# A short first load ahead of 64 KB runs in a streaming loss kernel

## The chip, the cores and the metric

The kernel runs on one core of one Trainium2 chip. The metric is the device time of one execution in microseconds. The profile's own span is some 1.3 us shorter (82.9 against 84.23 in the profiled run of the kernel before).

## The reference

```python
batch, dim = 1024, 4096            # log_input and target, float32
loss = np.exp(log_input) - target * log_input
return np.mean(loss, axis=-1).astype(np.float32)
```

Two inputs of 16.8 MB each are read once, and 4 KB are written.

## The kernel before

Partition p holds rows 8p to 8p+7, so eight rows of one partition lie one after another in HBM, 128 KB in all. ScalarE (ACT) does the exp with its row sum, VectorE (DVE) the product with its row sum, and all loads are issued by the sync engine (SP). The first load takes four rows of x at once: 128 runs of 64 KB, eight on each of the 16 transfer engines.

```python
    loads = []
    for first, rows in ((0, 4), (4, 2), (6, 1)):
        loads += [("x", first * d, rows * d), ("t", first * d, rows * d)]
    # ... the last row follows in seven ever smaller loads (TAIL)

    for i, (what, lo, w) in enumerate(loads):
        if what == "x" and lo in (6 * d, 7 * d):
            free = 1 if lo == 6 * d else 4
            nc.sync.wait_ge(exp_done, free)      # rows 6 and 7 reuse the first buffer
            nc.sync.wait_ge(prod_done, free)
        src = x_v if what == "x" else t_v
        dma = nc.sync.dma_start(out=place(what, lo, w), in_=src[:, lo : lo + w])
        dma.then_inc(landed[i] if i < len(loads) - 1 else last_ready, 16)
        if lo < 6 * d:
            early.append(dma.ins)
    before_first_barrier(nc, early)              # the first four issues go ahead of the barrier
```

Each load counts its semaphore up by 16, once per transfer engine, and the computing engines wait for 16. ACT starts when the first x load has landed, DVE when the first t load has.

## Time and profile before

| | before |
|---|---|
| device time, median of 3 | 84.14 us (83.91 to 84.20) |
| span of the profile | 82.9 us |
| HBM read | 33.55 MB, 405 GB/s over the span |
| first x load landed, first t load landed | 22.08 us, 41.41 us |
| DVE busy, ACT busy | 43%, 40% |

The transfers are the bound: DVE and ACT are idle more than half the time, and the last landing is followed only by about 2 us of computing and output. The page counts packets by size:

```profile
DMA packets 2016, 33.56 MB, mean 405 GB/s; under 512 B 352, under 2 KB 608, under 8 KB 1120
```

The second, of the timeline, is the exp table load, with its start, its length, and in brackets its wait:

```profile
2.97 1.28 ACT L155 ACT_TABLE_LOAD   x1 [2.97 <-PEq L48]
```

### The profile page before, as it was taken

Reading aid. Unit: us, or ns where it says so; the run is one execution under the profiler, and the core shown is the slowest. Engines: PE = TensorE matmul, PEld = TensorE weight load, DVE = VectorE, ACT = ScalarE, POOL = GpSimd, SP = SyncE. Lnnn points to the kernel's source line nnn. Section 1 sums busy time; section 2 is a strip of 40 time slices with the busy share of each in tenths; the row PEclk is TensorE's granted clock in tenths of the full one; section 3 lists DMA queues with packets and bytes.
Section 4 is the critical chain, followed back from the end, with each engine's and each line's share of the span. In section 5 each row is a group of like instructions: output and inputs, shape, how many; then the busy total and the mean of one; then the engine's idle time right before and its main releaser. Section 6 shows DMA issues by size and latency. Waiting matters only on the chain.

```text
span 82.9 us, 131 instructions
## 1 busy us (share of the span) xinstructions
DVE 35.6 (43%) x22; ACT 33.2 (40%) x35; POOL 0.3 (0%) x5
## 2 busy tenths in 40 slices
DVE  0000000000000000000099999999469996994992
ACT  0500000000399920000000897979793496019460
POOL 0000000000000000000000000000000000000000
DMA  9199999929999992999699799899899999999950
GB/s 506 63 443 506 506 506 506 443 127 443 506 506 506 506 443 127 443 506 506 269 490 474 316 474 490 380 411 490 364 403 435 443 435 393 433 397 421 393 184 2
DMA packets 2016, 33.56 MB, mean 405 GB/s; under 512 B 352, under 2 KB 608, under 8 KB 1120
## 3 DMA queue, kind: packets, MB, share of 16 engines
q1 hardware_dynamic: 2016, 33.56, 95.5%
HBM read 33.55 MB, written 0.00 MB: 405 GB/s over the span
## 4 chain that ended last, share of the span: by engine, by line
DMA 72%; DVE 18%; issue 4%; SPq 3%; ACT 1%
DMA t_big<-in_target_dram 49%; DMA x_big<-in_log_input_dram 23%; DVE t_big L175 17%; SPq L129 3%; DVE t_big L193 1%; ACT e_dump L155 1%; DVE parts L175 0%; SPq L127 0%; DVE all_loss L193 0%
## 5 line engine op out<-in xcount | busy, mean ns | idle before, releaser
L175 DVE CUSTOM_DVE_ANT_0 t_big<-t_big,x_big 128x4096 f32<-128x4096 f32 (+2 forms) x8 | 26.2, 3306 | 43.8 <-DMA t_big<-in_target_dram 43.6
L155 ACT ACTIVATE e_dump<-x_big 128x4096 f32<-128x4096 f32 (+3 forms) x8 | 21.8, 2730 | 24.2 <-DMA x_big<-in_log_input_dram 24.0
L175 DVE CUSTOM_DVE_ANT_0 t_mid<-t_mid,x_mid 128x4096 f32<-128x4096 f32 x2 | 8.8, 4424 | 2.0 <-DMA t_mid<-in_target_dram 2.0
L141 ACT ACTIVATE join_dump<-parts 128x2 f32<-128x2 f32 x7 | 1.4, 203 | 20.4 <-DVE parts L175 20.4
L155 ACT ACTIVATE e_dump<-x_mid 128x4096 f32<-128x4096 f32 x2 | 7.1, 3568 | 0.0
L155 ACT ACT_TABLE_LOAD x1 | 1.3, 1283 | 3.0 <-PEq L48 3.0
L155 ACT ACTIVATION_READ_ACCUMULATOR e_dump<-x_big 128x1 f32 x8 | 1.5, 186 | 0.0
L141 ACT ACTIVATION_READ_ACCUMULATOR join_dump<-parts 128x1 f32 x7 | 1.3, 186 | 0.0
L193 DVE CUSTOM_DVE_ANT_0 t_big<-t_big,x_big 128x390 f32<-128x390 f32 x1 | 0.6, 566 | 0.1
L175 DVE DVE_READ_ACCUMULATOR2_ANT parts<- 128x1 f32 x7 | 0.6, 81 | 0.0
L155 ACT ACTIVATION_READ_ACCUMULATOR e_dump<-x_mid 128x1 f32 x2 | 0.4, 186 | 0.0
L175 DVE DVE_READ_ACCUMULATOR2_ANT t_big<- 128x1 f32 x3 | 0.2, 83 | 0.0
L136 POOL MEMSET x_big<- 128x6 f32 x1 | 0.1, 103 | 2.5 <-POOLq L48 2.5
L227 POOL MEMSET const-bfloat16-1.0<- 128x1 bf16 x1 | 0.1, 101 | 0.0
L227 POOL MEMSET const-uint8-127<- 128x1 uint8 x1 | 0.1, 101 | 0.0
L227 POOL MEMSET const-float32-0.0<- 128x1 f32 x1 | 0.1, 98 | 0.2 <-issue 0.2
L227 POOL MEMSET const-float32-1.0<- 128x1 f32 x1 | 0.1, 98 | 0.0
L193 DVE DVE_READ_ACCUMULATOR2_ANT all_loss<- 128x1 f32 x1 | 0.1, 84 | 0.0
## 6 DMA issues: line engine op xcount, KB each, us to landing
x_mid<-in_log_input_dram SPq DMA_DIRECT2D x1, 4096.0 KB, 50.2
t_mid<-in_target_dram SPq DMA_DIRECT2D x1, 4096.0 KB, 59.5
x_big<-in_log_input_dram SPq DMA_DIRECT2D x1, 2048.0 KB, 19.8
t_big<-in_target_dram SPq DMA_DIRECT2D x1, 2048.0 KB, 24.3
x_big<-in_log_input_dram SPq DMA_DIRECT2D x1, 1536.0 KB, 15.3
t_big<-in_target_dram SPq DMA_DIRECT2D x2, 768.0 KB, 17.6
x_big<-in_log_input_dram SPq DMA_DIRECT2D x1, 384.0 KB, 18.8
t_big<-in_target_dram SPq DMA_DIRECT2D x1, 320.0 KB, 19.1
```

The lines of the kernel that those rows point to most:

```text
L129: dma = nc.sync.dma_start(out=place(what, lo, w), in_=src[:, lo : lo + w])
L136: nc.gpsimd.memset(big["x"][:, 4 * d : 4 * d + n_parts], -1.0).then_inc(ones_done, 1)
L141: nc.scalar.activation(out=join_dump[:, 2 * row : 2 * row + 2], in_=parts[:, 2 * row : 2 * row + 2], func=ACT_F.Copy, scale=inv_d, accum_o ...
L155: nc.scalar.activation(out=e_dump[:, col : col + w], in_=place("x", lo, w), func=ACT_F.Exp, bias=0.0, scale=1.0, accum_out=parts[:, 2 * ro ...
L175: nc.vector.tensor_tensor_reduce(out=place("t", lo, w), in0=place("t", lo, w), in1=place("x", lo, w), scale=-1.0, scalar=0.0, op0=ALU.mult ...
L193: nc.vector.tensor_tensor_reduce(out=place("t", lo, w + n_parts), in0=place("t", lo, w + n_parts), in1=place("x", lo, w + n_parts), scale= ...
L227: nc = _bacc.Bacc("TRN2", target_bir_lowering=False, num_devices=1)
```

## The change

The intent is to let the transfers start on something short: the first 256 columns (1 KB per partition, 128 KB in all) come by a load of their own, and a second load brings the remaining 63 KB of each 64 KB run. Both count up the same semaphore, so its users wait for 32.

```diff
+FIRST = 256
+    full = [32] + [16] * (len(loads) - 2)
-        dma = nc.sync.dma_start(out=place(what, lo, w), in_=src[:, lo : lo + w])
-        dma.then_inc(landed[i] if i < len(loads) - 1 else last_ready, 16)
-        if lo < 6 * d:
-            early.append(dma.ins)
+        sem = landed[i] if i < len(loads) - 1 else last_ready
+        cuts = [lo, lo + FIRST, lo + w] if i == 0 else [lo, lo + w]
+        for a, b in zip(cuts, cuts[1:]):
+            dma = nc.sync.dma_start(out=place(what, a, b - a), in_=src[:, a:b])
+            dma.then_inc(sem, 16)
+            if lo < 6 * d:
+                early.append(dma.ins)
 # ... and three waits on landed[...] take full[...] in place of 16
```

More of the change, by code (lines that the diff above doesn't have):

```diff
@@ L161 @@
             accum_out=parts[:, 2 * row : 2 * row + 1] if row < last_row else part(k - last_row),
-        ).wait_op(landed[i], 16, "sem-ge").then_inc(
+        ).wait_op(landed[i], full[i], "sem-ge").then_inc(
             exp_done if k < n_x - 1 else last_ready, 1
@@ L172 @@
         if j == 0 or x_load > t_work[j - 1][2]:
-            nc.vector.wait_ge(landed[x_load], 16)
+            nc.vector.wait_ge(landed[x_load], full[x_load])
         if j < n_t - 1:
@@ L185 @@
                 else part(n_x - last_row + j - last_row),
-            ).wait_op(landed[i], 16, "sem-ge").then_inc(
+            ).wait_op(landed[i], full[i], "sem-ge").then_inc(
                 prod_done if j < n_t - 2 else last_ready, 1
```

## The prediction

> **What bounds the kernel now.** I read the chain of waits first, because it says what the end hangs on; then the waits in order of cost; then the bytes and the busy share of the transfer engines in stretches that follow the landings; and last, in narrow stretches, the first ten microseconds, where the change acts.
>
> The page of the kernel before opens with the span, and its chain says what ended last:
>
> ```profile
> span 82.9 us, 131 instructions
> DVE 35.6 (43%) x22; ACT 33.2 (40%) x35; POOL 0.3 (0%) x5
> DMA 72%; DVE 18%; issue 4%; SPq 3%; ACT 1%
> HBM read 33.55 MB, written 0.00 MB: 405 GB/s over the span
> ```
>
> Both compute engines are busy under half of the span, and the chain is 72% transfer. 33.55 MB have to come in. What the chain's 18% of DVE hides is seen in its pieces in order of time, start and length first:
>
> ```profile
> 0.43 40.99 DMA t_big<-in_target_dram
> 41.44 4.42 DVE t_big L175
> 59.00 0.33 SPq L129
> 61.30 18.97 DMA x_big<-in_log_input_dram
> 80.28 0.02 issue
> 80.82 0.02 issue
> 80.84 0.57 DVE t_big L193
> ```
>
> The pieces from 41.44 to 59.00 are there only because the issue of the tail loads waits for a buffer; the queue is not empty meanwhile, as the next view shows. It cuts the span at the landings of the first x load (22.08), the first t load (41.41) and the middle t load (60.85); the last three columns are clock, busy share of the 16 transfer engines, and GB/s:
>
> ```profile
> 0.00:22.08 22.08, 0.00 (x0) 1.28 (x1) 0.30 (x5) 1.00 1.02 427
> 22.08:41.41 19.33, 0.00 (x0) 7.42 (x4) 0.00 (x0) 1.00 0.94 409
> 41.41:60.85 19.44, 17.47 (x8) 13.60 (x15) 0.00 (x0) 1.00 1.00 430
> 60.85:80.75 19.90, 17.55 (x12) 10.83 (x16) 0.00 (x0) 1.00 0.95 395
> ```
>
> A packet is booked where it starts, so shares lean between neighbours; the durations are the firmer reading. The first four rows of t, 8.39 MB, need 19.33 us (434 GB/s). The first four rows of x, the same bytes on an idle machine, land at 22.08, that is 2.75 us more. The stream never runs dry afterwards, and from the last landing only about 2 us of compute and output follow. So the end is: start-up of the transfers, plus 33.55 MB at the pace of the slowest transfer engine, plus a fixed tail. The change can only touch the first of these three.
>
> Where the 2.75 us go, by narrow stretches at the start, each of which holds the starts of 16 packets of 64 KB, one per transfer engine, or none:
>
> ```profile
> 0.90:1.70 0.80, 0.00 (x0) 0.00 (x0) 0.00 (x0) 1.00 3.97 1311
> 1.70:3.90 2.20, 0.00 (x0) 0.93 (x1) 0.10 (x1) 1.00 0.00 0
> 3.90:4.90 1.00, 0.00 (x0) 0.36 (x1) 0.00 (x0) 1.00 2.42 1049
> 4.90:6.30 1.40, 0.00 (x0) 0.00 (x0) 0.00 (x0) 1.00 0.00 0
> 6.30:7.30 1.00, 0.00 (x0) 0.00 (x0) 0.00 (x0) 1.00 2.42 1049
> ```
>
> Share times width, times 16 engines over 16 packets, is the mean time of one packet: 3.97 x 0.80 = 3.18 us in the first round, 2.42 x 1.00 = 2.42 us in the second and third. So the first round costs 0.76 us per engine above pace, and the first packets begin about 1.0 us after the first issue. 1.0 + 0.76 = 1.76 us; the last engine of the second round begins at about 4.83 where the mean is about 4.37, so another 0.45 us is the lag of one straggler, which it carries to the end because every engine then runs at one pace. 1.0 + 0.76 + 0.45 plus the spread of the first starts (the last at 1.64, mean 1.19, so 0.2 for the mean) is 2.4; the rest, about 0.35, is from the last byte to the landing seen by the waiter.
>
> [...] the first issue ends at 0.38 and packets begin at 1.0, so 0.62 us. [...] In the stretch 79.0 to 79.2, in the small tail loads, the trace has 73 packets (10 of them semaphore writes) at 377 GB/s with a busy share of 1.08, so 349 GB/s of busy time against 434 for 64 KB packets. [...]
>
> **The change part by part.**
> (1) Added: one more issue, 0.43 us on the sync engine's queue like its neighbours, before the first barrier. The later early issues move by 0.45 to 0.5 us (0.43 plus the 0.05 gap). The second t load is needed on the engines only at 21 us, so this is hidden. The barrier also moves, and with it the exp table load, now 2.97 to 4.25; its first user starts at 22.1. Nothing on the path.
> (2) Added: 128 packets of 1 KB, 8 on each engine. 131 KB at 349 GB/s are 0.375 us, where they took 131 KB / 434 = 0.302 us inside the long runs: +0.07 us on the path. One more semaphore write per engine is about 0.01.
> (3) Moved: the long runs shrink to 63 KB, 8 of them at 27.1 GB/s are 19.04 us instead of 19.33 us.
> (4) Moved: the start-up. First bytes flow where the first packet's end lies 2.42 us away: mean 4.35 - 2.42 = 1.93 us. The small packets are then written by about 1.93 + 0.375 = 2.3. The second load's descriptors come 0.47 us after the first's, so its reads begin at about 1.19 + 0.47 = 1.66 and, if they too need the full 0.76, give data at 2.42; if the path is warm by then, before 2.3. So the long runs flow from 2.3 to 2.42, where before the same byte flowed at 1.93 + 0.30 = 2.23. Sum of (2) to (4) for the mean engine: +0.07 to +0.19 us.
> (5) Moved: the straggler. The end is not that of the mean engine but of the last, 0.45 us behind. [...] I take half of the lag off as my central guess: about -0.25 us. That is a choice, not a reading.
> Center: +0.1 - 0.25 = -0.15 us, about 84.0 us.
>
> **The rivals.** First, that the 0.76 us are the crowding of sixteen 64 KB reads that start together, and not a latency. For it: engines that start late in the first round (1.62 and 1.64) are not late in the second. If small packets get through quickly and stagger the engines, the second load's first round is at pace and up to 0.35 us (all that its 0.47 us later start leaves: 1.66 against 1.19 + 0.76 + 0.07 is 0.36) comes off the mean engine, with the straggler 0.8 us: 83.3 us. Second, that the first long packet pays the 0.76 us in any case and the small load only stands ahead of it with a bubble: +0.2 us and a new straggler of the same size, 84.3 to 84.5 us. For it: the fill is paid per first 64 KB packet, and only 0.37 us of work lies ahead to hide it. Third, that nothing at the start counts since compute sets the end. Against it: the last x landing releases ACT at 80.30 and the last compute runs at 80.84, 0.1 us behind its data; a start-up gain passes through one to one. Fourth, a shift into the tail: tail loads are issued from 59.00 to 62.2 and reach the engines only at about 70, so even 1 us less start-up leaves no hole there.
>
> **Range and chances.** The whole that can be moved is 0.76 + 0.45 = 1.2 us, 1.4% of 84.14, so over 2% (1.68 us) faster would need more than all of it, and slower by 2% has no cause in sight: one issue and 0.07 us of packet cost. The three runs of before span 0.3 us, which I add on both sides. Predicted 84.0 us, 83.3 to 84.5 for 8 in 10; faster 3%, within 96%, slower 1%.
>
> **What would show it.** Right: the first x load complete at 21.6 to 22.2 us, the t load exactly 19.3 us behind it, the barrier and table load some 0.45 us later with nothing following from it, 144 more packets under 2 KB (128 of data and 16 semaphore writes), and unchanged 2.42 us rounds less 1/64. The first rival is right if the long packets' first round is at pace (2.38 us); the second if its mean is 3.1 us again. Wrong altogether: if the distance between the x and the t landing changes, as then the change acts on the steady pace, which I hold impossible; or if the first four rows land more than 1.2 us earlier, as then the 0.62 us before the first packet also depends on the size.

## The result, and the profile after

| | before | after |
|---|---|---|
| device time, median of 6 runs each | 84.06 us (83.91 to 84.20) | 84.19 us (84.04 to 84.50) |
| ratio | | 1.0018, interval 0.9996 to 1.0039 |
| the change again (6 and 11 runs) | 83.96 us | 84.31 us, ratio 1.0044, interval 1.0021 to 1.0068 |

A ratio is the mean time of one kernel's runs over that of the other's in the same rounds, so it is not quite the ratio of the two medians. Executions over 1.5% slower than the fastest of the same kernel are left out of the means. The difference is far under 2%. Taking both together, the change costs 0.2 to 0.4%, some 0.15 to 0.35 us; only the second interval stands clear of 1. A ratio of 1.0012 to 1.003 was expected, or 0.9993 to 1.0007 if there was no cost; 1.0044 lies above both.

The profile after is that of an 84.50 us run, the slowest of the six, 0.31 us above their median. Its span and packet count, of the page:

```profile
span 83.2 us, 132 instructions
...
DMA packets 2160, 33.56 MB, mean 404 GB/s; under 512 B 368, under 2 KB 752, under 8 KB 1264
```

Its table load, of the timeline:

```profile
3.43 1.28 ACT L163 ACT_TABLE_LOAD   x1 [3.43 <-PEq L52]
```

And pieces of its chain of waits in order of time (start, length):

```profile
0.90 40.81 DMA t_big<-in_target_dram
...
41.73 4.43 DVE t_big L183
...
61.62 18.92 DMA x_big<-in_log_input_dram
80.54 0.02 issue
...
81.11 0.57 DVE t_big L201
```

There are 144 packets more, all of them under 2 KB. The barrier and with it the table load moved by 0.46 us, which matters to nobody. The t landing, and everything in the chain behind it, moved by 0.3 us from 41.41 to 41.71, and the last compute by the same 0.27 us from 80.84 to 81.11. So nothing was gained or lost between 41 us and the end; the whole of this difference arises before the first t load has landed.

Stretches at the start of the same profile (from:to, width, busy time of the engines, clock, busy share of the 16 transfer engines, GB/s):

```profile
0.90:1.49 0.59, 0.00 (x0) 0.00 (x0) 0.00 (x0) 1.00 0.57 165
1.49:2.60 1.11, 0.00 (x0) 0.00 (x0) 0.00 (x0) 1.00 2.83 960
4.40:5.40 1.00, 0.00 (x0) 0.32 (x1) 0.00 (x0) 1.00 2.38 1032
```

In the third stretch all 16 second long packets start: 2.38 x 1.00 = 2.38 us each, the pace for 63 KB. The first long packets sit in the second stretch together with the last small ones. The packet records themselves give 3.04 us for them in the mean, 0.66 us over pace. The small packets had gone through in mostly 44 to 46 ns each, and the first long packet of an engine was slow all the same.

Because the last engine decides the time (before, the last increment is at 41.41 us and DVE starts at 41.44) and its lag differs from trace to trace (0.18 to 1.08 us in the table below), I use two figures from each trace below, worked out from its semaphore records (no view prints them). The **mean landing** is the mean of the sixteen semaphore increments of the first t load, which all sixteen engines reach at full pace (2.42 us for 64 KB) after the same bytes: 40.94 us before, 41.14 us after. The **lag** is the last increment minus that mean: 0.47 us before, 0.57 us after.

### The profile page after: what moved, and what is told of

Read it like the earlier page. It is cut to its first block, busy times and chain, and to the rows that moved or that the text cites. A ratio compares the mean times of both kernels' runs of the same rounds, so it can differ in the third digit from the quotient of the medians.

```text
span 83.2 us, 132 instructions
## 1 busy us (share of the span) xinstructions
DVE 35.6 (43%) x22; ACT 33.2 (40%) x35; POOL 0.3 (0%) x5
## 4 chain that ended last, share of the span: by engine, by line
DMA 72%; DVE 18%; issue 5%; SPq 4%; ACT 1%
DMA t_big<-in_target_dram 49%; DMA x_big<-in_log_input_dram 23%; DVE t_big L183 17%; SPq L137 4%; DVE t_big L201 1%; ACT e_dump L163 1%; DVE parts L183 0%; SPq L132 0%; DVE all_loss L201 0%
```

## The experiments

### The dose: 64, 512 and 1024 columns, and three loads of 256

```diff
-FIRST = 256
+FIRST = 64        # and 1024, and 512 in two later calls
```
```diff
-        cuts = [lo, lo + FIRST, lo + w] if i == 0 else [lo, lo + w]
+        cuts = [lo, lo + FIRST, lo + 2 * FIRST, lo + 3 * FIRST, lo + w] if i == 0 else [lo, lo + w]
```

The theory after the result: the second issue comes 0.47 us after the first (0.43 us of issue and the gap); the small load occupies an engine for less than that, then the engine runs dry, and the first long packet pays the whole start-up of about 0.7 us. What the small load gives back is its bytes. The rival: there is no cost, only the scatter of the slowest engine.

64 columns:

> The first load brings 64 columns (256 B per partition, 2 KB per transfer engine) in place of 256. Theory A (the long runs begin one issue, 0.47 us, later, and the small load pays back only the bytes it moved: 2 KB per engine are 0.08 us): 0.39 us slower than the kernel before, about 84.45 us. Rival D (the change costs nothing and the 0.13 us seen are scatter of the slowest engine): equal to the kernel before within 0.15 us.

1024 columns:

> The first load brings 1024 columns (4 KB packets, 32 KB per engine, 1.2 us of work), so the second load's descriptors are there before the first load is done. Theory A: the issue gap is covered, the time is that of the kernel before within 0.15 us; the slow start of about 0.7 us is paid once, somewhere in the first 4 KB packets or at the first long packet. If the excess sits in the small packets and the long ones run at pace from the first, it is a cost of the first tens of KB; if the long ones show it again, it belongs to long reads starting together. Rival D: equal to the kernel before as well; the profile alone tells here.

Three loads of 256:

> Three loads of 256 columns go ahead of the rest of the long runs, where the change has one. Theory A: the long runs begin 3 x 0.47 = 1.41 us later and 3 x 0.30 = 0.90 us of bytes are already in, so 0.5 us slower than the kernel before, about 84.55 us. Rival D: equal within 0.15 us.

512 columns, and again:

> 512 columns: 16 KB per engine, 0.60 us of work, just over the 0.47 us of the second issue. Theory A: the long runs no longer start from idle, mean landing of the first t load as before within 0.1 us, time 0 to 0.1 us above before. If instead the start-up is again paid by the first long packets, the gap of 0.47 us is not the reason, and the time is that of the change, 0.2 to 0.3 us above before.

> 512 columns once more, as it was the only width that came out under the kernel before (ratio 0.9985, interval 0.9959 to 1.0011). If the start-up of the transfers runs partly under the 2 KB packets, the mean landing of the first t load is again 0.1 to 0.2 us earlier than in the two profiles of the kernel before (40.94 and 40.90 us), and the ratio 0.998 to 0.9995; if it was scatter, 0.9995 to 1.001.

Measured, with the kernel before at 84.01 us in each of these calls except the two of the change (84.06 and 83.96 us).

| first load | median | ratio (interval) | mean landing | lag |
|---|---|---|---|---|
| none (before; control) | 84.01 us | | 40.94; 40.90 us | 0.47; 0.22 us |
| 64 columns | 84.46 us | 1.0051 (1.0037 to 1.0065) | 41.35 us | 0.28 us |
| 256 columns, the change | 84.19; 84.31 us | 1.0018; 1.0044 | 41.14; 41.07 us | 0.57; 0.25 us |
| 3 x 256 columns | 85.13 us (85.33 with the slow run) | 1.0143 (1.0104 to 1.0181) | 41.69 us | 1.08 us |
| 512 columns | 83.98; 83.86 us | 0.9985; 0.9994 (0.9959 to 1.0011; 0.9973 to 1.0014) | 40.76; 40.77 us | 0.30; 0.18 us |
| 1024 columns | 84.07 us | 1.0005 (0.9993 to 1.0018) | 40.87 us | 0.27 us |

The rival falls: 64 columns cost 0.43 us where 0.39 was expected, clear of 1. The order is as the theory has it: with 8 KB per engine or less ahead of the gap there is a cost, with 16 or 32 KB (0.60 and 1.2 us of work, more than the gap of 0.47 us) there is none. One rival is left untested: the size of the packets (256 B to 4 KB) grew together with the bytes per engine, and no run brought 16 KB in packets of 1 KB by one load.

Where the start-up sits shows best in the kernel with 1024 columns. Three narrow answers of its transfer view; "DMA packets" counts what starts in the stretch, and the second line is the busy share, as a sum over 16 engines. First 0.90 to 1.70:

```profile
DMA packets 20, 0.08 MB, mean 102 GB/s; under 512 B 0, under 2 KB 0, under 8 KB 20
...
q1 hardware_dynamic: 20, 0.08, 103.5%
```

Then 2.20 to 2.70, where there are only 4 KB packets too:

```profile
DMA packets 54, 0.22 MB, mean 442 GB/s; under 512 B 0, under 2 KB 0, under 8 KB 54
...
q1 hardware_dynamic: 54, 0.22, 109.2%
```

And 2.80 to 3.35, where the 16 long packets start, with 16 semaphore writes and 16 more of 4 KB:

```profile
DMA packets 48, 1.05 MB, mean 1907 GB/s; under 512 B 16, under 2 KB 16, under 8 KB 32
...
q1 hardware_dynamic: 48, 1.05, 442.7%
```

The first 4 KB packets took 1.035 x 0.80 x 16 / 20 = 0.66 us each, the later ones 1.092 x 0.50 x 16 / 54 = 0.16 us. In the last stretch there are 4.427 x 0.55 x 16 = 38.96 us of engine time; without 16 packets of 0.16 us and 16 semaphore writes of 0.01 us, 36.3 us are left for 16 long packets, 2.27 us each. That is exactly the pace for 60 KB. So here the start-up is paid by the first packets of the short load, and the long packets begin at pace. This is what the change was meant to do, and its 1 KB packets do not do. But paid early or late, it is paid: 1024 columns gain 0.03 to 0.07 us in the mean landing and nothing in the time.

The same sum for whole starts, each from one line. For the change (0.90 to 2.60) and for 512 columns (0.90 to 2.50):

```profile
q1 hardware_dynamic: 160, 1.16, 204.9%
```
```profile
q1 hardware_dynamic: 160, 1.28, 219.0%
```

Each holds all small packets and the first long one of every engine. The change: 2.049 x 1.70 = 3.48 us per engine for 72,704 bytes, which are 2.68 us at the 27.1 GB/s of one engine (64 KB in 2.42 us); 0.80 us over pace. 512 columns: 2.190 x 1.60 = 3.50 us for 79,872 bytes, 2.95 us at pace; 0.56 us over. The kernel before had 3.18 - 2.42 = 0.76 us. The second profiles of the same three kernels give 0.75, 0.57 and, for the kernel before, 0.68 us. So with 512 columns a part of the start-up is indeed saved, and the mean landing is 0.13 to 0.19 us earlier in both profiles than in both of the kernel before, more than I had expected of it; its long packets were still 0.29 and 0.19 us over pace. The time follows only as a tendency: both ratios are under 1, and neither interval excludes it. It is the only width that may beat the kernel before, by a tenth of a per cent.

The packet records of all widths can be summed up in one estimate: the mean end of the first long packets, less their length at pace, is when the long data flow. With 64, 256 and 512 columns that is 2.40, 2.42 and 2.34, and 2.34 and 2.35 us, always 1.50 to 1.56 us after the end of that load's issue, and so it is in both profiles of the kernel before (1.93 and 1.89 us, 1.55 and 1.51 us after the issue). So up to 512 columns the small load leaves the long load's own start-up about as long as it was; it delays it by one issue and gives back its bytes. (Outside this range lie three loads with 1.74 us and, further down, the load from ACT's queue with 1.42 and 1.44 us. With 1024 columns the engines are busy with the small load until 3.0 us.) That engines run dry is plain only with 64 columns (by the records 2.5 to 8.7 of 16 are at work between 1.3 and 1.9 us); with 256 it is 12.4 or more from 1.6 us on.

Three loads were dearer than expected (84.55 us expected, 85.13 measured in the fast runs). In the mean landing they are 0.74 us late where 0.5 was predicted, and the last engine is 1.08 us behind the mean. The first long packets of the other engines ended between 5.39 and 5.92 us, of the last two at 6.55 and 6.96 us. The sum at the start (141.5% over 3.10 us, 4.39 us per engine for 87,040 bytes) is 1.18 us over pace: 0.69 us of it in the first long packets, the rest in the small ones, which took 57 ns in the mean, hardly more than the 54 ns of the change. The long packets began 1.67 us later than in the kernel before, not 1.41; why, and why two engines fall so far behind, isn't known.

### Crowding: how many engines start at once

```diff
+        cuts = [0, 2, 6, 14, 16, P] if i == 0 else [0, P]     # first try: neighbouring partitions
+        cuts = [8, 16, 32, P] if i == 0 else [P]              # second: every fourth partition of these
+            if k > 0:
+                dma.wait_op(sem, 16 * k, "sem-ge")            # each load waits for the one before
```

> The first x load is cut by partitions into loads of 2, 4, 8, 2 and 112 partitions, each waiting for the one before, so that 2, 4, 8, 2 and 16 transfer engines start from idle with 64 KB packets (pace 2.42 us). Theory A (crowding: sixteen long reads that start together slow each other): the first packet is near pace with 2 engines (excess under 0.2 us), grows with 4 and 8, and is about 0.7 us over pace with 16. Rival B (a fixed fill time for every long packet that starts on an idle engine): excess 0.65 to 0.8 us in every step. Rival C (a one-time cost of the first touch): excess only in the first step, near 0 in the last. The time is some 10 us longer in all three; it decides nothing.

The first try (126.73 us, result correct) decides nothing about crowding. Its stretches for the steps of 2, 4 and 8 engines:

```profile
0.90:1.00 0.10, 0.00 (x0) 0.00 (x0) 0.00 (x0) 1.00 5.55 1311
7.30:7.90 0.60, 0.00 (x0) 0.00 (x0) 0.00 (x0) 1.00 1.93 437
14.20:14.80 0.60, 0.00 (x0) 0.00 (x0) 0.00 (x0) 1.00 6.67 874
```

Share x width x 16 / packets: 4.4 us with 2, 4.6 with 4, 8.0 with 8. This looks like crowding, but even two engines alone were slow, 4.4 us against 2.42 us at pace. In the step of 8 the quickest packet took 6.94 us and the slowest 8.96. All these packets go to neighbouring partitions, whose rows are 128 KB apart in HBM. In steps one to three of the second try the partitions lie 4 apart, and so their rows 512 KB; the two are not separated:

> Mended ladder: before the whole first x load, loads of 2, 4 and 8 partitions that lie 4 apart, each waiting for the one before, so that 2, 4, 8 and at last 16 transfer engines start from idle with 64 KB packets [...]. Theory A1 (crowding of engines): the first packet's excess over 2.42 us is under 0.2 us with 2 engines and grows to about 0.7 with 16. Rival B (each engine's own fill time): 0.6 to 0.8 us in every step. The time is some 12 us longer either way.

It gave 99.52 us, result correct. The starts of the first packets of 2, 4, 8 and 16 engines, and the second packets of the 16:

```profile
1.50:1.60 0.10, 0.00 (x0) 0.00 (x0) 0.00 (x0) 1.00 4.25 1311
6.60:7.50 0.90, 0.00 (x0) 0.00 (x0) 0.00 (x0) 1.00 0.84 291
11.70:12.40 0.70, 0.00 (x0) 0.00 (x0) 0.00 (x0) 1.00 2.15 749
16.40:17.50 1.10, 0.00 (x0) 0.00 (x0) 0.00 (x0) 1.00 2.70 953
19.50:20.20 0.70, 0.00 (x0) 0.23 (x1) 0.00 (x0) 1.00 3.46 1498
```

The first packet takes 3.40 us with 2 engines, 3.02 with 4, 3.01 with 8, 2.97 with 16, and 2.42 us at pace. The excess is 0.98, 0.60, 0.59 and 0.55 us. It does not grow with the number of engines: the crowding theory, first rival of the prediction and my own first explanation, falls. Eight engines, which took 8.0 us in the mean with neighbouring partitions, took 3.0 us with partitions four apart; the cause of that was not shown. Whether each engine pays a start-up of its own is not shown. In the step with 8 engines, seven started together and one later:

```profile
11.70:12.10 0.40, 0.00 (x0) 0.00 (x0) 0.00 (x0) 1.00 3.38 1147
12.30:12.40 0.10, 0.00 (x0) 0.00 (x0) 0.00 (x0) 1.00 1.53 655
```

The seven took 3.38 x 0.40 x 16 / 7 = 3.09 us, the late one 1.53 x 0.10 x 16 = 2.45 us, nearly at pace. In the traces of before and after, too, the engines that start last are among those with the least excess: before, those that start at 1.62 and 1.64 us took 2.91 and 2.76 us (mean 3.18); after, those that start at 2.34 and 2.55 us took 2.67 and 2.82 us (mean 3.04). This fits a start-up that is counted from the issue of the load, as in the estimate above; no run tests it.

### Warm or cold: the long runs after the short load has landed

```diff
+            if k > 0:
+                dma.wait_op(sem, 16 * k, "sem-ge")            # rest waits for the 256 columns
```

> As the change, but the rest of the long runs waits until the 256 columns have landed. Theory A (the start-up is paid by the first long packets whatever small load went ahead): their excess is again 0.6 to 0.8 us, and the time about 85.6 us (the long runs start some 1.4 us later than with the change). Rival C (a one-time cost of the first touch, which the small load takes on itself once it has landed): long packets at pace, 2.38 us, and about 84.9 us.

It took 85.85 us in its one run (state unknown; about 85.6 expected), beside 83.96 us before. The first long packets start in the first stretch, the second ones in the other:

```profile
3.00:4.10 1.10, 0.00 (x0) 0.00 (x0) 0.00 (x0) 1.00 2.82 938
5.90:6.80 0.90, 0.00 (x0) 0.40 (x1) 0.00 (x0) 1.00 2.65 1147
```

2.82 x 1.10 = 3.10 us against 2.65 x 0.90 = 2.39 us: 0.72 us of start-up in full, although 128 KB had come by the same queue a microsecond earlier. It isn't a cost of the first touch that this short load had taken on itself. In the mean of the engines it was there in every start from idle that was traced, in the ladder four times in a row (0.98, 0.60, 0.59 and 0.55 us).

### The split without the delay: the short load from ACT's queue

```diff
+            small = i == 0 and a == 0
+            queue = nc.scalar if small else nc.sync            # the long runs are SP's first issue again
```

> The 256 columns are issued from ACT's queue at the start, and the rest of the long runs is the first issue of the sync queue, as the whole load was before. The split and its 144 packets stay, the delay of the long runs goes. Theory A: the time is that of the kernel before within 0.1 us (ratio 0.999 to 1.001). Rival E (the 144 small packets themselves, or the scatter that they bring, are the cost): 0.15 us slower as with the change.

> The small load from ACT's queue once more. Theory A with the packet overhead of 0.07 to 0.08 us from the prediction: ratio about 1.001. Rival E: about 1.003, as the change.

Measured: 84.13 us, ratio 1.0017 (1.0000 to 1.0034), and 84.15 us, ratio 1.0010 (0.9984 to 1.0036). The timing doesn't decide between 1.001 and 1.003 by itself, nor does it tell these runs from the first of the change (1.0018); the first ratio lies just above what I had allowed. What was run is also not quite what its name says. From 0.90 to 3.90 us of the first profile only the 16 long packets start:

```profile
DMA packets 16, 1.03 MB, mean 344 GB/s; under 512 B 0, under 2 KB 0, under 8 KB 0
```

The first 1 KB packet starts at 4.00 us, after the first long packet of its engine, and the others follow one by one between the long packets. So this tests the split and its 144 packets without the delay, not a short load that goes ahead. The traces say more: the mean landing is 40.92 and 40.89 us, that of the kernel before and not the 41.07 to 41.14 us of the change. So at 41 us no cost of the split is left once the long runs are issued first; what the time keeps above 84 us, if anything, comes later. In the second profile (an 84.54 us run) the last x load landed at 80.58 us, 0.3 us later than in the first profile of before, although the first t load had landed 0.2 us earlier: there is scatter in the later loads too (the mean of its landing marks fell 0.5 us behind that of the kernel before between 51 and 74 us).

### The control

> The kernel before, unchanged, as if it were a change: how far the method and the scatter of the slowest engine go by themselves. Ratio 0.9985 to 1.0015. Its profile is a second look at the lag of the last engine behind the mean, 0.47 us at the landing of the first t load in the first profile; I expect another value between 0.2 and 0.5, as the profile of before that was shown was the slowest of its three runs.

84.05 us, ratio 1.0002, interval 0.9974 to 1.0031, wider than I had expected because single runs reached 84.47 and 84.58. Its chain shows the t load landing 0.29 us earlier than in the first profile of the same kernel:

```profile
0.43 40.70 DMA t_big<-in_target_dram
```

Between these two profiles of one kernel the mean landing differs by 0.04 us and the lag by 0.25 us. So a difference of 0.1 to 0.3 us at a last landing, in a single profile, says nothing.

## Why the prediction was right or wrong

The range (83.3 to 84.5), the class and the main ground for both held: the end is start-up plus bytes at a fixed pace (the t load lands 19.33 us behind the x load before, 19.36 us after) plus a fixed tail, and only the start-up can move. By the steps of the prediction:

1. **The extra issue is hidden.** Right: the table load moved from 2.97 to 3.43 us, and its first user still waited for data at 22 us.
2. **Packet cost +0.07 us.** Somewhat low. The change's start took 3.48 us per engine; without the 3.04 us long packet and the semaphore write, 0.43 us are left for eight small packets instead of 0.375, so +0.13 us over the 0.302 us inside long runs. Eight of the median packet (46 ns) would be 0.37 us; a few slow ones, up to 0.26 us, make the rest.
3. **Shorter runs.** Right: second rounds of 2.38 us.
4. **The start-up of the long runs, +0.07 to +0.19 us for the mean engine together with 2 and 3.** It was an estimate from the first two rounds of the trace (1.93, 0.47 and 0.76 us). Right at its upper end, which stood for a full second payment: the mean landing went from 40.94 and 40.90 us to 41.14 and 41.07 us, 0.13 to 0.24 us. The long packets' excess was 0.66 us (0.64 us in the second profile), and the restart shows that a landed small load does not lessen it. By the packet records the long data flow from 2.42 and 2.34 us, where the step gave 2.30 to 2.42. One part of its picture was wrong: the small packets were not held back until 2.3 us, the last of them started at 1.73 us.
5. **Half of the straggler's lag comes off, -0.25 us.** This step failed, and it turned the sign. The lag was 0.57 and 0.25 us with the change, 0.47 and 0.22 us without; it was not halved. The 0.45 us that I had taken as a property of the kernel was that of a single profile. The step was marked as a choice, and it should have been zero: then the sum is +0.1 to +0.2 us, about 84.2 us, which is what came. The center forecast a gain and a loss came; that the measured time lies within the range all the same is due to the range's width, and is no merit of this step.

One of the signs that were named for "right" failed in the first profile: the first x load was complete at 22.35 us (21.97 in the second), outside 21.6 to 22.2. The t load followed 19.36 and 19.35 us later, as foretold.

Of the rivals, the second is what happened (start-up paid by the long packets in any case, 84.3 to 84.5 us given, 84.19 and 84.31 us measured). The first, crowding, is refuted by the ladder. The evidence I had cited for it (late engines show less excess) shows up in the ladder with 8 engines too (2.45 us for the late one, 3.09 us for the other seven), where no crowding was found, so it isn't evidence for crowding.

Open: what the 0.7 us consist of. They are not charged to eight 1 KB packets (54 ns each in the mean, and the long packet behind them still 0.66 us over pace), are charged partly to eight of 2 KB (the long packet 0.29 and 0.19 us over), and almost wholly to the first of eight 4 KB packets (0.66 us, the later ones 0.16 us). By estimate from these figures they are met after the first few KB of a stream; no run here shows what they are. Open as well is what makes single engines late.

## What to carry to other kernels

In this kernel a short load ahead of a long one cost time when its bytes kept each transfer engine busy for less than its extra issue delayed the long load, 0.47 us; by estimate that is 12.7 KB per engine at the measured 27.1 GB/s (8 KB and 16 KB were measured, nothing between). Below it the delay was lost in part or in full, 0.43 us with 2 KB and 0.15 to 0.35 us with 8 KB; above it the split was free (ratios 0.9985 and 0.9994 with 16 KB, 1.0005 with 32 KB), and the start-up, at 0.6 to 0.7 us of 84, was not worth much more effort. When the slowest of sixteen engines ends a kernel, take the mean of its landing marks to see a mechanism of a tenth of a microsecond, and never read one from the last mark of one profile: two profiles of one kernel differed there by 0.29 us, in the mean by 0.04 us.
